# A projection's ends pinned in program order, and the C B product of each group moved three gemms later

## The chip, the core and the metric

The kernel runs on one core of a Trainium2 chip. Five engines work side by side: PE (TensorE) multiplies matrices into PSUM, DVE (VectorE) and ACT (ScalarE) do elementwise work, POOL (GpSimd) small copies, and SP (SyncE) issues most of the transfers. The metric is the device time of one execution in microseconds, the median of several runs. The profile shows one execution of its own.

## What is computed

One layer of a hybrid block on a sequence of 256 rows of width 2048, all in fp32: dilated attention with 16 heads beside a state-space (SSM) part with 8 groups of 8 heads, their branches gated, merged, projected and normalized. What matters here is the projection and the SSM part:

```python
hn = rms_norm(x, norm_w)
proj = hn @ w_in
q, k, v, z_a, z_s, xbc, dt_raw, g_a, g_s = jnp.split(proj, split_points, axis=-1)
...
xbc = jax.nn.silu(causal_depthwise_conv(xbc, conv_w, conv_b))
xs, bm, cm = jnp.split(xbc, [SSM_INNER, SSM_INNER + SSM_GROUPS * SSM_STATE], axis=-1)
dt = jax.nn.softplus(dt_raw.astype(jnp.float32) + dt_bias.astype(jnp.float32))
...
acum = jnp.cumsum(dac, axis=1)
decay = jnp.exp(jnp.where(causal, seg, -jnp.inf))
cb = jnp.einsum('blgn,bsgn->bgls', cc, bc)
y_diag = jnp.einsum('bgls,bgjls,bsgjp->blgjp', cb, decay, xc)
```

The kernel treats the two chunks of 128 rows as one triangle of three blocks, so that no state is carried: C B is made once for a group and multiplied by the decays of its eight heads.

## The kernel before

**Weights.** All weights stream once, in units of 128 x 1024 (L267 to L281). Of each unit ACT makes the rounded part `h` (L276) and DVE the rest `l` (L277); four of each are buffered. The activations XT lie there as a high and a low half side by side.

**Projections.** `gemm_a` (L320 to L333), called by `project`, makes one tile of 128 output columns over 16 steps `kt`. Each step has one product of `h` with both halves of XT (512 columns, L329) and one of `l` with the high half (256 columns, L332): 32 products in one PSUM bank. `gates` uses another form, `gemm_b`.

**Order.** The program is traced in one order, and a scheduler then orders the instructions of each engine anew, by priority and by when it takes each to be ready. Only what goes through `in_order` (`keep_in_program_order`, L200) is fixed: that instruction stays behind the last one traced before it on its engine. Before the change that holds for the products of the scan (L819).

**Ticks.** Each gemm begins with a `tick` (L316). `after(n, f)` puts a piece of work n ticks on. It runs when that gemm's tick comes, ahead of its first product; with a last argument of 1 it runs half a tick later, at L331, between the first and the second product of the gemm. What is due together runs in the order of due times.

**The SSM part.** In front come a first block of four tiles (`gemm_first`, four ticks), dt (one tick) and two gates of four ticks each. Then each group g has the gemms B and C (not group 0) and four times `xs` and `zs` (group 0 has three of each here, xs1 to zs3). What stands between:

- `dt_chain` (L704), on DVE, some thirty dependent small steps from dt_raw to the running sum `ac_t` (two scans, L733), all in the tile `early`. It is put nine ticks behind dt. When it runs it puts `dt_turn` (L737) DT_LAG = 2 ticks on: four transposes `dt_tp` (L742), the copies dtT and acT (L743, L744) and a product `lastb` (L746) that reads acT.
- `make_cb` (L766): the C B product of a group, in two products of plain fp32 (L768, L769, two passes each), and its masking on DVE (L770). It is put CB_LAG ticks behind the group's C, half a tick in; for group 0 at a place of its own (L890).
- `decays` (L772): ACT makes the decays of a group from `acb` and acT, DVE multiplies by cb (L791).
- `turn` (L793): eight transposes `xtp` (L801) of the group's `xs`, TURN_LAG = 3 ticks behind its last `xs`; that is in front of the next group's C.
- `scan` (L811): 16 products `yp` (L820, two passes each), half a tick into a later gemm. For group g that gemm is the last `zs` of group g + 1. `gather` (L828) follows on DVE and ACT.
- `conv`, `evac` and `half_silu` end each projection on ACT and DVE (L761, L383, L385, L387, L396, L397).

**The attention** uses `gemm_a` for q, k and za of 16 heads; `scores`, `turn_p` and `mix` come by ticks.

Of the kernel before, what the change touches and what calls it, by code (L numbers as in the profile page):

```python
# [16 lines left out]
S = 256  # L17
# [6 lines left out]
KT = D // P  # L24
# [9 lines left out]
X_CUTS = ((0, 1), (1, 2), (2, 4), (4, 6), (6, 8), (8, 10))  # L34
N_FINE = 4
N_ACT_X = 1
DT_LAG, CB_LAG, TURN_LAG, GT_LAG, Y_LAG, S_LAG, M_LAG = 2, 5, 3, 2, 11, 2, 2
Y_AFTER = 0, 0
GS_BEFORE = {0: (0, 1), 4: (2,)}
A_ORDERS = {0: (0, 1, 2, 4, 3, 6, 5, 7), 2: (0, 2, 1, 4, 3, 5, 6, 7)}  # L40
# [156 lines left out]
def hybrid_block(ctx: ExitStack, tc: tile.TileContext, wall, xt, x, pk_d, cst_d, fw_d, out):  # L197
    nc = tc.nc
    ve, ac, gp, pe = nc.vector, nc.scalar, nc.gpsimd, nc.tensor
    in_order = tc.keep_in_program_order  # L200
# [23 lines left out]
    def bank(tag, bufs, name):  # L224
        return ps.tile([P, 512], F32, name=name, tag=tag, bufs=bufs)
# [41 lines left out]
    def unit(n, shape):  # L267
        if n not in loaded:
            load(n)
        w = loaded.pop(n)  # L270
        h = stream.tile([P, UNIT], F32R, name=f"h{n}", tag="h", bufs=H_BUFS)
        l = stream.tile([P, UNIT], F32R, name=f"l{n}", tag="l", bufs=H_BUFS)
        cuts = (0, UNIT // 2, UNIT) if n < N_FINE else (0, UNIT)
        with tc.high_priority(L_AHEAD) if n >= KT // UB else nullcontext():
            for a, b in zip(cuts, cuts[1:]):
                ac.activation(h[:, a:b], w[:, a:b], AF.Copy)  # L276
                ve.tensor_tensor(l[:, a:b], w[:, a:b], h[:, a:b].bitcast(F32), ALU.subtract)  # L277
        for f in on_unit.pop(n, ()):
            f(h[:, 0:1].bitcast(F32))
        k, m = shape  # L280
        return h.rearrange("p (k m) -> p k m", k=k), l.rearrange("p (k m) -> p k m", k=k)  # L281
# [25 lines left out]
    def run_due(until):  # L307
        while True:
            ready = [d for d in due if d[0] <= until]
            if not ready:  # L310
                break
            d = min(ready, key=lambda e: e[0])
            due.remove(d)
            d[1]()

    def tick(final=False):  # L316
        now[0] += 1
        run_due(float("inf") if final else now[0])

    def gemm_a(tag, xs_of, acc=None):  # L320
        tick()
        name = f"{tag[0]}{tag[1]}"
        acc = bank(acc, 2, f"ps_{name}") if acc else bank("g", 4, f"ps_{name}")
        for u in range(KT // UK):
            h, l = unit(FIRST[tag] + u, (UK, P))
            for kk in range(UK):
                kt = u * UK + kk
                m = xs_of(kt)
                pe.matmul(acc, h[:, kk, :], m, start=(kt == 0), stop=False)  # L329
                if kt == 0:  # L330
                    run_due(now[0] + 0.5)  # L331
                pe.matmul(acc[:, S:], l[:, kk, :], m[:, :S], start=False, stop=(kt == KT - 1))  # L332
        return acc  # L333

    def gemm_dt(src):
# [23 lines left out]
    def project(tag, acc=None):  # L359
        return gemm_a(tag, lambda kt: XT[:, kt, :], acc)  # L360
# [324 lines left out]
    with tc.tile_pool(name="ssm", bufs=2) as sp:  # L685
# [223 lines left out]
        for g in range(GROUPS):  # L909
# [9 lines left out]
            for t in range(max(4 * g, 1), 4 * g + 4):  # L919
                u, i = divmod(t, 2)  # L920
                acc = project(("xs", t))
# [19 lines left out]
                acc = project(("zs", t))  # L941
# [330 lines left out]
```

## Time and profile before

| what | us |
|---|---|
| median of 3 runs | 1385.39 |
| lowest, highest | 1384.93, 1388.81 |
| span of the profiled execution | 1383.8 |
| PE busy in it | 1373.6 |
| DVE busy | 1169.5 |
| ACT busy | 835.5 |

The profiled execution's own time is its span, from the first to the last instruction, 1383.8 us. A row of the timeline gives the start in us, the time taken in us, engine, line, operation, the tile written and the tiles read, shapes and a count. Matmuls overlap in the pipeline: the distance of two starts is what a product costs, the time in its row is longer. A plain fp32 product shows as two matmuls. A row of the windows gives a stretch, its length, the busy time of each engine asked for with the number of instructions, the granted clock of PE, the share of the DMA engines and GB/s. A row of the groups gives the count, then busy time and mean duration in ns, then the idle time of the engine ahead of them with what ended it.

### The profile page before, as it was taken

How to read it: one execution, taken by the hardware profiler on the slowest of the kernel's cores; microseconds unless marked ns; L12 is line 12 of the kernel's file. 1: busy time of each engine (PE TensorE's matmuls, PEld its weight loads, DVE VectorE, ACT ScalarE, POOL GpSimd, SP SyncE). 2: the span in 40 equal slices, each digit the busy share in tenths (PEclk: the TensorE clock that was granted, in tenths of full speed). 3: DMA queues.
4: the chain of work that ended last, by engine and by line, in shares of the span. 5: the costliest groups of instructions: out<-in, count | busy, mean ns of one | idle time of the engine just before them, and what ended most of it. 6: DMA issues, size and time to landing. Idle time of an engine off the chain costs nothing.

```text
span 1383.8 us, 20696 instructions
## 1 busy us (share of the span) xinstructions
PE 1373.6 (99%) x7266; PEld 1169.9 (85%) x7266; DVE 1169.5 (85%) x1753; ACT 835.5 (60%) x1306; POOL 142.0 (10%) x226
## 2 busy tenths in 40 slices
PE   9999999999999999999999999999999999999997
PEld 8888888888888888888888888888888888888886
DVE  7898999987799898789889897777877788888897
ACT  7656677675667675766565554544544556655564
POOL 2301111101011100010001001111111000000112
PEclk9999999999999999999999999999999999999999
DMA  9767988868787866668677668888888757865773
GB/s 347 231 187 225 313 254 291 279 224 287 245 266 240 294 212 208 188 224 280 230 259 267 222 209 278 275 275 273 299 288 301 241 161 264 294 222 180 243 273 122
DMA packets 105080, 345.00 MB, mean 249 GB/s; under 512 B 11728, under 2 KB 13712, under 8 KB 104976
## 3 DMA queue, kind: packets, MB, share of 16 engines
q1 hardware_dynamic: 103536, 339.62, 74.0%
q10 hardware_dynamic: 1440, 4.06, 0.8%
q8 instruction: 57, 0.93, 0.3%
q14 instruction: 47, 0.39, 0.1%
HBM read 314.87 MB, written 28.77 MB: 248 GB/s over the span
## 4 chain that ended last, share of the span: by engine, by line
PE 97%; DMA 1%; DVE 1%; ACT 1%; issue 0%; SPq 0%; POOL 0%; POOLq 0%; DVEq 0%; ACTq 0%
PE ps_zs L329 8%; PE ps_xs L329 8%; PE ps_zs L332 4%; PE ps_q L329 4%; PE ps_za L329 4%; PE ps_k L329 4%; PE ps_xs L332 4%; PE ps_ssm L476 3%; PE ps_ssm L477 3%; PE ps_ssm L478 3%; PE ps_q L332 2%; PE ps_k L332 2%; PE ps_za L332 2%; PE ps_gs L414 2%; PE ps_gs L412 2%; PE ps_gs L413 2%
## 5 line engine op out<-in xcount | busy, mean ns | idle before, releaser
L276 ACT ACTIVATE h<-w 128x1024 fp32r<-128x1024 f32 (+1 forms) x398 | 413.9, 1047 | 318.0 <-issue 78.8
L277 DVE TENSOR_TENSOR l<-w,h 128x1024 fp32r<-128x1024 f32 (+1 forms) x398 | 479.4, 1211 | 124.2 <-ACT h L276 121.8
L329 PE MATMUL ps_zs<-XT,h 128*128 128x512 f32 x496 | 176.3, 397 | 0.0
L329 PE MATMUL ps_xs<-XT,h 128*128 128x512 f32 x496 | 175.9, 396 | 0.0
L332 PE MATMUL ps_zs<-XT,l 128*128 128x256 f32 x496 | 139.9, 282 | 0.0
L332 PE MATMUL ps_xs<-XT,l 128*128 128x256 f32 x496 | 139.8, 282 | 0.0
L329 PEld LDWEIGHTS ps_xs<-XT,h 128*128 128x128 f32 x496 | 93.3, 188 | 21.7
L329 PEld LDWEIGHTS ps_zs<-XT,h 128*128 128x128 f32 x496 | 93.4, 188 | 21.2
L332 PEld LDWEIGHTS ps_zs<-XT,l 128*128 128x128 f32 x496 | 93.7, 189 | 1.5 <-issue 0.7
L332 PEld LDWEIGHTS ps_xs<-XT,l 128*128 128x128 f32 x496 | 93.7, 189 | 0.4
L329 PE MATMUL ps_q<-XT,h 128*128 128x512 f32 x256 | 92.5, 405 | 0.2 <-ACT h L276 0.2
L329 PE MATMUL ps_k<-XT,h 128*128 128x512 f32 x256 | 89.9, 395 | 0.0
L329 PE MATMUL ps_za<-XT,h 128*128 128x512 f32 x256 | 89.7, 394 | 0.0
L543 ACT ACTIVATE ha<-wa 128x1024 fp32r<-128x1024 f32 x43 | 45.4, 1055 | 46.4 <-DMA wa<-in_wall 10.9
L332 PE MATMUL ps_q<-XT,l 128*128 128x256 f32 x256 | 71.2, 278 | 0.0
L332 PE MATMUL ps_k<-XT,l 128*128 128x256 f32 x256 | 71.1, 278 | 0.0
L332 PE MATMUL ps_za<-XT,l 128*128 128x256 f32 x256 | 71.1, 278 | 0.0
L544 DVE TENSOR_TENSOR la<-wa,ha 128x1024 fp32r<-128x1024 f32 x43 | 52.5, 1220 | 11.9 <-ACT ha L543 11.8
L782 ACT ACTIVATE gt<-acb,acT 128x128 f32<-128x128 f32 x128 | 44.2, 391 | 23.7 <-DMA acb<-acum_d 21.9
L329 PEld LDWEIGHTS ps_q<-XT,h 128*128 128x128 f32 x256 | 48.2, 188 | 11.5 <-ACT h L276 0.6
L329 PEld LDWEIGHTS ps_za<-XT,h 128*128 128x128 f32 x256 | 48.1, 188 | 11.3
L329 PEld LDWEIGHTS ps_k<-XT,h 128*128 128x128 f32 x256 | 48.1, 188 | 11.2
(688 smaller groups left out, 3325.1 us busy)
## 6 DMA issues: line engine op xcount, KB each, us to landing
w<-in_wall SPq DMA_DIRECT2D x394, 512.0 KB, 4.7
wa<-in_wall SPq DMA_DIRECT2D x43, 512.0 KB, 4.9
th_a<-in_wall SPq DMA_DIRECT2D x19, 512.0 KB, 5.6
sums_at<-in_wall SPq DMA_DIRECT2D x18, 512.0 KB, 4.7
acb<-acum_d SPq DMA_DIRECT2D x32, 256.0 KB, 4.0
t_ssm<-sums_at SPq DMA_DIRECT2D x13, 512.0 KB, 4.1
wt<-t_ssm SPq DMA_DIRECT2D x13, 512.0 KB, 5.4
th_a<-in_wall SPq DMA_DIRECT2D x19, 256.0 KB, 6.0
```

The source lines that it names most:

```text
L276: ac.activation(h[:, a:b], w[:, a:b], AF.Copy)
L277: ve.tensor_tensor(l[:, a:b], w[:, a:b], h[:, a:b].bitcast(F32), ALU.subtract)
L329: pe.matmul(acc, h[:, kk, :], m, start=(kt == 0), stop=False)
L332: pe.matmul(acc[:, S:], l[:, kk, :], m[:, :S], start=False, stop=(kt == KT - 1))
L412: pe.matmul(accs[i], xh, h[:, kk], start=(kt == 0), stop=False)
L413: pe.matmul(accs[i], xh, l[:, kk], start=False, stop=False)
L476: pe.matmul(acc, xh, h, start=start, stop=False)
L477: pe.matmul(acc, xh, l, start=False, stop=False)
L478: pe.matmul(acc, xl, h, start=False, stop=stop)
L543: ac.activation(h, src, AF.Copy)
L544: ve.tensor_tensor(l, src, h.bitcast(F32), ALU.subtract)
L782: ac.activation(g4[:, n, b], acb[:, j, b // 2 * P : b // 2 * P + P], AF.Relu, scale=-1.0, bias=sc[:, h : h + 1],)
```

## The change

CB_LAG goes from 5 to 8: the C B product of groups 1 to 7 is now due in the gemm in which the scan of the group in front is due, and is traced behind that scan. In `gemm_a` the first product (`h` of step 0) and the last (`l` of step 15) go through `in_order`. The first is so held behind the last PE instruction that was traced before it, which may be one of the tick's own; the last behind the product ahead of it.

```diff
-DT_LAG, CB_LAG, TURN_LAG, GT_LAG, Y_LAG, S_LAG, M_LAG = 2, 5, 3, 2, 11, 2, 2
+DT_LAG, CB_LAG, TURN_LAG, GT_LAG, Y_LAG, S_LAG, M_LAG = 2, 8, 3, 2, 11, 2, 2
...
                 m = xs_of(kt)
-                pe.matmul(acc, h[:, kk, :], m, start=(kt == 0), stop=False)
+                ends = [pe.matmul(acc, h[:, kk, :], m, start=(kt == 0), stop=False)]
                 if kt == 0:
+                    in_order(ends[0])
                     run_due(now[0] + 0.5)
-                pe.matmul(acc[:, S:], l[:, kk, :], m[:, :S], start=False, stop=(kt == KT - 1))
+                ends.append(pe.matmul(acc[:, S:], l[:, kk, :], m[:, :S], start=False, stop=(kt == KT - 1)))
+                if kt == KT - 1:
+                    in_order(ends[1])
```

## The prediction

> **What bounds the kernel now.** I read the page first: the engines, then the chain that ended last.
>
> ```profile
> span 1383.8 us, 20696 instructions
> ...
> PE 1373.6 (99%) x7266; PEld 1169.9 (85%) x7266; DVE 1169.5 (85%) x1753; ACT 835.5 (60%) x1306; POOL 142.0 (10%) x226
> ...
> PE 97%; DMA 1%; DVE 1%; ACT 1%; issue 0%; SPq 0%; POOL 0%; POOLq 0%; DVEq 0%; ACTq 0%
> ```
>
> The reader is to see that PE is never without work and that 97% of the last chain is PE. So an edit pays only if PE spends fewer microseconds on the same products, and any time for which PE is made to wait is lost whole: no slack anywhere absorbs it. A page that says 99% cannot show waits that do not exist yet. So next I went through the timeline of PE and, since the change fixes PE's order, that of the engines whose results PE would then have to wait for.
>
> **The C B products.** The timeline of PE, at the product of group 1 and at the scan of group 0:
>
> ```profile
> 146.87 0.59 PE L768 MATMUL cbp<-ct,bt 128*128 128x256 f32 x2
> 147.30 0.39 PE L769 MATMUL cbp<-ct,bt 128*128 128x128 f32 x2
> 147.65 0.39 PE L329 MATMUL ps_xs<-XT,h 128*128 128x512 f32 x1
> ...
> 164.24 0.40 PE L329 MATMUL ps_zs<-XT,h 128*128 128x512 f32 x1
> 164.57 2.82 PE L820 MATMUL yp<-gt,xdt 128*64 128x256 f32 x32
> 167.32 0.39 PE L332 MATMUL ps_zs<-XT,l 128*128 128x256 f32 x1
> 167.54 0.39 PE L329 MATMUL ps_zs<-XT,h 128*128 128x512 f32 x1
> ```
>
> From the first cbp to the next `h` product are 0.78 us, of which an `l` product would take 0.12 anyway (16 pairs take 5.54 in the window at 124.46 below, 0.35 a pair, and an `h` 0.23, 247.90 to 248.13): the detour costs 0.66 us. Its two passes over 256 columns take 0.43 (146.87 to 147.30), and two over 128, at half of that, 0.22: 0.65. So only some 0.01 us is a price of changing over and could be saved by standing elsewhere. The scan's detour is 164.24 to 167.54 less one `h` (0.23) and one `l` (0.12), 2.95 us; a change-over can be in it, at its end (0.22 for the `l` after it, not 0.12, and as much again before). If the C B product shared that end it would save up to 0.2 us a group, 1.4 for the seven groups 1 to 7; if passing from the scan's 64-column tiles to 128 costs a second time, it loses 0.1 each, 0.7. I take **0**, by the row of cbp itself, and keep −1.4 and +0.7. Nothing late follows on DVE: the result's first reader, L791 of the same group, comes two gemms (11 us) after the new place, and L770 (0.55 us) only moves.
>
> **The pace of the projections.** Gemms of 32 equal products do not all take equally long. The windows that hold one gemm each, one of each kind:
>
> ```profile
> 76.79:82.43 5.64, 5.64 (x16) 2.94 (x16) 1.00 0.60 193
> ...
> 124.46:130.00 5.54, 5.54 (x17) 3.00 (x17) 1.00 0.65 218
> ```
>
> 0.10 us apart at the same granted clock (1.00). Following the starts through the part, the pace changes only at interruptions. Behind each transpose (xtp) it is the short one; behind the cbp at 146.87 and those of groups 3 to 7 the long one; behind every scan the long one; and mostly also where the first product of a `zs` gemm stands inside the `xs` gemm before it:
>
> ```profile
> 247.90 0.40 PE L329 MATMUL ps_xs<-XT,h 128*128 128x512 f32 x1
> 248.13 0.39 PE L329 MATMUL ps_zs<-XT,h 128*128 128x512 f32 x1
> 248.37 0.28 PE L332 MATMUL ps_xs<-XT,l 128*128 128x256 f32 x1
> ```
>
> By those starts some 40 of the 70 gemms of groups 1 to 7 run at the long pace. The change takes the cbp away from the middle of the group and forbids the stray first product, so that only what stands between a scan and the next transposes (a `zs` and a `B`, some 12 gemms in all) should stay long. 28 gemms times 0.105: **−2.9 us**, between −4.2 (all 40) and +3.2 (the other 30 become long). Why the pace changes the trace does not show; I take it as a regularity. The Trainium skill, "TensorE: Matmul & The Clock Gate", "Wait — 56ns, not 53.3ns?", has a fixed 2.5 ns per matmul above N ÷ 2.4 GHz, whatever stood before; by it this term would be 0 and the sum 2.9 us higher, but the two kinds of window above disagree with a fixed gap.
>
> **The pinned products.** In front of `xs2` (the third `xs` tile, group 0) `tick` runs `dt_turn`: `dt_chain` is due nine ticks after the first gemms; the two gates take eight, so that is `xs1`, and DT_LAG is 2. `dt_turn` issues four transposes and then `lastb` (L746), which reads acT. Pinned behind the last PE instruction written before it, the first product of `xs2` will stand behind `lastb`. Now the transposes drift:
>
> ```profile
> 88.08 0.40 PE L329 MATMUL ps_xs<-XT,h 128*128 128x512 f32 x1
> ...
> 111.76 0.39 PE L329 MATMUL ps_B<-XT,h 128*128 128x512 f32 x1
> 112.08 0.33 PE L742 MATMUL dt_tp<-cst,early 64*128 64x64 f32 x2
> 112.35 0.70 PE L768 MATMUL cbp<-ct,bt 128*128 128x256 f32 x2
> ...
> 113.47 0.39 PE L332 MATMUL ps_B<-XT,l 128*128 128x256 f32 x1
> ...
> 118.78 0.33 PE L746 MATMUL lastb<-acT,cst 128*128 128x64 f32 x2
> 118.95 1.05 PE L801 MATMUL xtp<-cst,xs 128*128 128x128 f32 x8
> ```
>
> `xs2` starts at 88.08, `lastb` at 118.78, 30 us later. That is no idle choice of place, for DVE ends the chain late:
>
> ```profile
> 108.72 0.73 DVE L733 TENSOR_TENSOR_SCAN early<-early 64x128 f32<-64x128 f32 x2
> 109.38 1.19 DVE L277 TENSOR_TENSOR l<-w,h 128x1024 fp32r<-128x1024 f32 x1
> ...
> 114.22 0.28 DVE L743 COPY dtT<-dt_tp 128x128 f32<-128x128 f32 x1
> 114.41 0.28 DVE L744 COPY acT<-dt_tp 128x128 f32<-128x128 f32 x1
> ```
>
> So PE will stop at 88.08. Everything on PE is behind that product: the rest of `xs2`, and each later projection by its own pin. Only cbp of group 0 may go ahead. How long? While PE stands, DVE has less to do. DVE's windows, first the chain's tile `early` alone up to its end and up to 97.70, then all of DVE up to 97.70, and the groups of that stretch that need `xs2`:
>
> ```profile
> 88.10:109.50 21.40, 5.87 (x17) 1.00 0.67 189
> 88.10:97.70 9.60, 2.06 (x6) 1.00 0.66 187
> ...
> 88.10:97.70 9.60, 9.37 (x21) 1.00 0.66 187
> ...
> L277 DVE TENSOR_TENSOR l<-w,h 128x1024 fp32r<-128x1024 f32 x3 | 3.6, 1214 | 0.0
> ...
> L385 DVE TENSOR_TENSOR raw_x<-ps_xs,lo_x 128x256 f32<-128x256 f32 x1 | 0.4, 417 | 0.0
> ```
>
> The chain needs 5.9 us more of DVE in 17 dependent steps. Beside it DVE did 9.37 − 2.06 = 7.3 us; of these two of the three L277 (2.4) and L385 (0.4) wait for a buffer or a bank that only `xs2` frees, which leaves 4.5 us, plus L770 of the cbp that went ahead, 0.55. These gaps between dependent steps are filled one for one in the trace, so I count all of it: 88.1 + 5.9 + 4.5 + 0.5 = 99.0. Behind it come the last transposes (0.34), L743 and L744 (0.5), `lastb` and three handovers, some 0.5: 1.3. PE resumes at 100.2: **+12.1 us**. If the chain goes first it is 7.2.
>
> PE then restarts slow. The groups of the first 7.2 us, and PE's windows at the end of the run:
>
> ```profile
> L623 PE MATMUL warm<-ssq 128*128 128x256 f32 x8 | 3.8, 654 | 1.4 <-DVE ssq L620 1.4
> L377 PE MATMUL ps_first<-yTa,h 128*128 128x512 f32 x4 | 2.3, 718 | 0.0
> ...
> 1375.00:1379.50 4.50, 0.50 (x5) 1.00 0.71 260
> 1379.50:1383.80 4.30, 0.00 (x0) 0.50 0.60 215
> ```
>
> The granted clock falls to 0.50 some 4 us after the last matmul, and at the start products of 512 columns take 718 ns, not 400 (164.24), for the first 5.8 us (1.4 to 7.2). Half of 5.8 is 2.9; none if the few transposes in the stop keep the clock up. I take **+2.0**. The Trainium skill, "TensorE: Matmul & The Clock Gate", "What's actually happening", puts both the idle window and the slow restart at about 3.4 us; by that the term would be an estimated 1.7, and the sum 0.3 lower.
>
> In return the detours at 112.08 (113.47 − 111.76 less 0.23: 1.48) and of `lastb` at 118.78 (0.17) are gone from their old place, since they lie inside the stop: **−1.65**.
>
> The other pins bind little. Each C gemm is now behind the transposes of the group before, which need the last `xs`:
>
> ```profile
> 178.49 0.40 PE L329 MATMUL ps_C<-XT,h 128*128 128x512 f32 x1
> ...
> 178.15 0.42 DVE L397 SCALAR_TENSOR_TENSOR xs<-th_x,cv_x 128x256 f32<-128x256 f32 x1
> ...
> 824.90 0.50 PE L329 MATMUL ps_q<-XT,h 128*128 128x512 f32 x1 [0.20 <-ACT h L276]
> ...
> 824.90:832.90 8.00, 3.25 (x17) 1.00 0.85 291
> ```
>
> For group 1 that ends at 178.57, where C now begins at 178.49: some 0.2 us with the handover, and at most that in the six later groups. At 824.90 a product of the first q gemm fills a hole of the v gemm; pinned, it cannot, 0.3 us. The other q products in that window, all 17 together 3.25 us, stand among v's too, though no wait of v shows there. The attention's small products stand at gemm boundaries already. **+0.5**, from 0 to 4.6 (1.4 + 3.25).
>
> **Sum** against the profiled execution: 12.1 + 2.0 − 1.65 − 2.9 + 0.5 + 0 = +10.05; 1383.8 becomes 1393.85. The median is 1.6 us above that span, so the time is **1395.4 us**.
>
> **Rivals.**
> *The chain goes first.* DVE serves the 17 steps before the fillers (they were written earlier) and the clock holds: 7.2 − 1.65 − 2.9 + 0.5 = +3.2, 1388.6 us. For it: where no filler was ready (108.34 on) steps follow each other in 0.4 us. Against: up to 105 us each pair of steps has others between. 0.11.
> *No stop, faster.* The pin binds nothing long, because the chain is ended by the time `xs2` begins. It decides there: at 88.1 or before, the stop is nil. What stays is pace −2.9, the four gemms of group 0 short too −0.4, the shared end of the scan −1.4, pins +0.3: 1381.0 us. Against: 17 steps are left at 88.1, and nothing in the change touches what comes earlier. 0.14.
> *The pace does not follow.* The stop comes as forecast, but the long pace stays or spreads, by the skill's rule above 0 and at the far bound +3.2: with 0, 1398.3 us; up to 1401.5. 0.08.
> *The forecast*: 0.67.
>
> **The numbers.** A measurement here tells 0.3%, 4.2 us, from no change. Faster: 0.09 of the second rival. Same: its other 0.05 and 0.07 of the first, 0.12. Slower: 0.67, 0.04, 0.08, 0.79. The forecast's terms run from a stop of 7.2 to 13.5 and a pace of −4.2 to 0, so the range is 1386.5 to 1401; it takes in the first rival and most of the third and leaves out the second and the tails, 0.2.
>
> **What would show it.** In the profile after: PE idle before the first product of `xs2` for some 12 us, released by DVE or by `lastb`, with dt_tp and lastb right before it and DVE's L733 near 99; a granted clock under 1.00 there; cbp right behind yp with no gap and no saving; C, `xs` and `zs` at 5.55 a gemm, `zs` and `B` behind the scan at 5.65. No idle PE at 88 would fell the forecast; a stop with gemms still at 5.65 would fell the pace term alone.

## The result and the profile after

| | before | after |
|---|---|---|
| median of 4 runs, us | 1385.7 | 1398.74 |
| lowest, highest | 1384.93, 1388.81 | 1398.64, 1400.24 |
| span of the profiled execution | 1383.8 | 1397.0 |

The kernel became slower: the ratio of after to before is 1.0095, with an interval from 1.0081 to 1.0109. The forecast of 1395.4 had the sign and the main cause; the span grew by 13.2 us where the sum said 10.05. (In the changed kernel the `l` product's line is L333, not L332, and every line behind `gemm_a` has a number higher by three: L742, L746, L768, L801, L820 are now L745, L749, L771, L804, L823.)

The page of the changed kernel, engines, the clock in 40 slices, and the chain that ended last:

```profile
span 1397.0 us, 20700 instructions
...
PE 1373.7 (98%) x7266; PEld 1169.3 (84%) x7266; DVE 1171.0 (84%) x1753; ACT 837.9 (60%) x1306; POOL 148.5 (11%) x226
...
PEclk9989999999999999999999999999999999999999
```

PE has the same busy time as before, 1373.7 against 1373.6 us, in a span 13 us longer. That is misleading on its own, since slow products count as busy: a gain in one place and a loss in another cancel in the sum. The third slice, with a clock of 8 tenths, says where to look first. The timeline of PE there (start, duration, engine, line, operation, tiles, and in brackets the idle time in front with its releaser):

```profile
88.00 0.28 PE L333 MATMUL ps_zs<-XT,l 128*128 128x256 f32 x1
97.94 0.44 PE L745 MATMUL dt_tp<-cst,early 64*128 64x64 f32 x2 [9.65 <-DVE early L730]
98.31 1.22 PE L771 MATMUL cbp<-ct,bt 128*128 128x256 f32 x2
99.32 0.64 PE L772 MATMUL cbp<-ct,bt 128*128 128x128 f32 x2
99.89 0.47 PE L745 MATMUL dt_tp<-cst,early 64*128 64x64 f32 x2
101.00 0.69 PE L749 MATMUL lastb<-acT,cst 128*128 128x64 f32 x2 [0.64 <-DVE acT L747]
101.45 0.77 PE L329 MATMUL ps_xs<-XT,h 128*128 128x512 f32 x1
...
130.76 0.28 PE L333 MATMUL ps_B<-XT,l 128*128 128x256 f32 x1
133.82 1.10 PE L804 MATMUL xtp<-cst,xs 128*128 128x128 f32 x8 [2.78 <-DVE xs L400]
134.67 0.48 PE L329 MATMUL ps_C<-XT,h 128*128 128x512 f32 x1
```

There are **two stops**. The first is the forecast one: the stream of products ends at 88.12 (88.00 and the 0.12 of an `l`), and `xs2` starts at 101.45, behind `lastb`, 13.3 us later. The second was not forecast: 2.95 us between the end of the B gemm of group 1 (130.88) and the transposes of group 0's `xs`, behind which the C gemm of group 1 is now pinned.

The end of the chain on DVE:

```profile
98.21 0.73 DVE L736 TENSOR_TENSOR_SCAN early<-early 64x128 f32<-64x128 f32 x2
...
100.66 0.28 DVE L747 COPY acT<-dt_tp 128x128 f32<-128x128 f32 x1
```

It ends at 98.94, where the forecast had 99.0. From there to `xs2` it takes 2.5 us, not 1.3: PE serves the C B product of group 0 between the two halves of the transposes, from 98.31 to 99.89, and at half clock (0.50 from 97.9 to 101.4).

The windows of the changed kernel (length, then busy time and instructions of PE, PEld, DVE, ACT and POOL, the granted clock, DMA share, GB/s), at both stops:

```profile
88.10:101.40 13.30, 3.01 (x12) 2.15 (x11) 11.48 (x32) 2.98 (x6) 0.23 (x2) 0.62 0.31 92
101.40:108.60 7.20, 7.20 (x34) 6.25 (x34) 1.45 (x2) 2.88 (x7) 0.00 (x0) 0.76 0.23 73
...
130.80:133.80 3.00, 0.24 (x2) 0.00 (x0) 3.00 (x6) 1.86 (x4) 0.10 (x1) 1.00 0.92 296
```

The second row is the gemm `xs2`: 7.20 us at a clock of 0.76, 1.65 more than a gemm at the short pace. The last row shows that a stop of 3 us leaves the clock at 1.00. PE is idle for 10.3 us of the first row (13.30 less 3.01) and for 2.8 of the last: that is the 13 us by which the span grew, and the slow products and the quicker ones cancel in the busy time.

What feeds the second stop is ACT. Its timeline, then that of DVE:

```profile
104.13 0.70 ACT L785 ACTIVATE gt<-acb,acT 128x128 f32<-128x128 f32 x2 [10.00 <-DMA acb<-acum_d]
...
109.05 0.70 ACT L785 ACTIVATE gt<-acb,acT 128x128 f32<-128x128 f32 x2 [2.04 <-DMA acb<-acum_d]
...
120.48 0.70 ACT L785 ACTIVATE gt<-acb,acT 128x128 f32<-128x128 f32 x2 [2.83 <-DMA acb<-acum_d]
```

```profile
123.34 1.23 DVE L277 TENSOR_TENSOR l<-w,h 128x1024 fp32r<-128x1024 f32 x1 [3.92 <-ACT h L276]
...
133.34 0.42 DVE L400 SCALAR_TENSOR_TENSOR xs<-th_x,cv_x 128x256 f32<-128x256 f32 x1
```

While PE stands at 88, ACT comes to the decays of group 0, which need `acb`, a transfer that starts only when the chain has written ac_t (SP stores it at 98.97 and issues the first `acb` at 100.95). ACT works in order, so the weights' `h` (L276) stand behind that wait; DVE then stands for `h` (3.92 us before 123.34), and the last `xs` of group 0 is done at 133.76. The transposes start at 133.82.

What the change won is in the scan and behind it. The timeline of PE at scan 0, then PE's windows of three gemms, `xs` of group 1, `B` behind scan 0 and `xs` of group 2:

```profile
179.97 0.40 PE L329 MATMUL ps_zs<-XT,h 128*128 128x512 f32 x1
180.30 2.82 PE L823 MATMUL yp<-gt,xdt 128*64 128x256 f32 x32
183.05 0.70 PE L771 MATMUL cbp<-ct,bt 128*128 128x256 f32 x2
183.58 0.39 PE L772 MATMUL cbp<-ct,bt 128*128 128x128 f32 x2
183.72 0.36 PE L333 MATMUL ps_zs<-XT,l 128*128 128x256 f32 x1
183.93 0.40 PE L329 MATMUL ps_zs<-XT,h 128*128 128x512 f32 x1
```

```profile
140.40:146.05 5.65, 5.65 (x35) 1.00 0.68 217
189.13:194.68 5.55, 5.55 (x34) 1.00 0.72 209
201.11:206.65 5.54, 5.54 (x34) 1.00 0.71 237
```

The joint detour is 183.93 − 179.97 less an `h` (0.23) and an `l` (0.12): 3.61 us, as before for scan and C B product apart (2.95 + 0.66). Standing together saves nothing. But the `B` gemm behind it (189.13) runs at the short pace, and so does `xs` of group 2 (201.11). The `xs` of group 1 (140.40) is still long: it follows the second stop.

### The profile page after: what moved, and what is told of

It reads as the page before. It is cut to its first block, busy times and chain, and to the rows that moved or that the text cites. A ratio compares the mean times of both kernels' runs of the same rounds, so it can differ in the third digit from the quotient of the medians.

```text
span 1397.0 us, 20700 instructions
## 1 busy us (share of the span) xinstructions
PE 1373.7 (98%) x7266; PEld 1169.3 (84%) x7266; DVE 1171.0 (84%) x1753; ACT 837.9 (60%) x1306; POOL 148.5 (11%) x226
## 4 chain that ended last, share of the span: by engine, by line
PE 94%; DVE 2%; DMA 1%; ACT 1%; issue 1%; SPq 0%; POOL 0%; POOLq 0%; ACTq 0%; DVEq 0%
PE ps_xs L329 8%; PE ps_zs L329 8%; PE ps_k L329 4%; PE ps_za L329 4%; PE ps_q L329 4%; PE ps_xs L333 4%; PE ps_zs L333 4%; PE ps_ssm L480 3%; PE ps_ssm L481 3%; PE ps_ssm L479 3%; PE ps_q L333 2%; PE ps_k L333 2%; PE ps_za L333 2%; PE ps_gs L416 2%; PE ps_gs L417 2%; PE ps_gs L415 2%
## 5 line engine op out<-in xcount | busy, mean ns | idle before, releaser
L276 ACT ACTIVATE h<-w 128x1024 fp32r<-128x1024 f32 (+1 forms) x398 | 414.3, 1049 | 310.3 <-issue 78.1
L333 PE MATMUL ps_zs<-XT,l 128*128 128x256 f32 x496 | 138.8, 280 | 0.0
L333 PE MATMUL ps_xs<-XT,l 128*128 128x256 f32 x496 | 138.7, 280 | 0.0
L333 PEld LDWEIGHTS ps_xs<-XT,l 128*128 128x128 f32 x496 | 94.1, 190 | 0.0
L333 PEld LDWEIGHTS ps_zs<-XT,l 128*128 128x128 f32 x496 | 93.4, 188 | 0.0
L333 PE MATMUL ps_q<-XT,l 128*128 128x256 f32 x256 | 71.1, 278 | 0.0
L333 PE MATMUL ps_k<-XT,l 128*128 128x256 f32 x256 | 71.0, 278 | 0.0
L333 PE MATMUL ps_za<-XT,l 128*128 128x256 f32 x256 | 71.0, 277 | 0.0
L547 DVE TENSOR_TENSOR ltu<-wa,htu 128x1024 fp32r<-128x1024 f32 x38 | 46.4, 1222 | 15.6 <-ACT htu L546 15.6
```

Of the source, the lines that this page charges most:

```text
L333: ends.append(pe.matmul(acc[:, S:], l[:, kk, :], m[:, :S], start=False, stop=(kt == KT - 1)))
L547: ve.tensor_tensor(l, src, h.bitcast(F32), ALU.subtract)
```

## The experiments

Theory **A**: the loss comes from the pin on `xs2`'s first product, through both stops, the second being a consequence of the first; the lag of the C B product costs nothing. Its rival **B**: the moved C B product brings a part of the loss, or the many other pins do. All ratios are to the kernel before on the same chip; one us is 0.07%.

### The lag alone

```diff
-DT_LAG, CB_LAG, TURN_LAG, GT_LAG, Y_LAG, S_LAG, M_LAG = 2, 5, 3, 2, 11, 2, 2
+DT_LAG, CB_LAG, TURN_LAG, GT_LAG, Y_LAG, S_LAG, M_LAG = 2, 8, 3, 2, 11, 2, 2
```

The kernel before, with only this.

> The change with its lag alone: CB_LAG 8, no pin in the projections. Theory A (the loss of 13.0 us is made by the pins: PE is held at xs2 behind lastb and at the first C behind the transposes): no stop, PE idle under 0.5 us between 76 and 150, and a time within 3 us of before (1383 to 1388), the difference being the pace of the gemms, 0.105 us for each that turns long or short. Theory B (the moved C B product costs, because it waits or makes others wait behind the scan): 1390 us or more. The detour of scan and C B product together should take 3.6 us as in the changed kernel.

Measured: 1385.87 us, ratio 1.0004 [0.9995, 1.0012]. No stop, and no gain. The lag is without fault, and also without use when alone. The timeline of PE shows one reason, at the C B product of group 1:

```profile
147.65 0.39 PE L329 MATMUL ps_xs<-XT,h 128*128 128x512 f32 x1
147.87 0.59 PE L768 MATMUL cbp<-ct,bt 128*128 128x256 f32 x2
148.31 0.38 PE L769 MATMUL cbp<-ct,bt 128*128 128x128 f32 x2
148.44 0.36 PE L332 MATMUL ps_xs<-XT,l 128*128 128x256 f32 x1
```

The scheduler draws it ahead of the scan (165.57) by 18 us, to its old place, since nothing pins it. In the six other groups it does stand behind the scan, and the pace is short there; but the stray first products of the next gemm are still there, and in four groups (3, 5, 6 and 7) the first of them is where the pace turns long again.

### The pins alone

The changed kernel with CB_LAG back at 5.

> The pins alone, CB_LAG back at 5. Theory A: the stop at xs2 of about 13.3 us and the slow restart of about 1.65 us stay, the second stop at the first C too (about 2.9 us): 1397 to 1401 us. Theory B: near before, 1384 to 1388. Besides: if the C B product is what turns the pace long, the gemms from xs2 of a group to its scan take 5.65 us here, and the time is 1 to 3 us above the changed kernel's 1398.7.

Measured: 1399.47 us, ratio 1.0101 [1.0088, 1.0115]. The loss is all in the pins. PE's timeline has the first stop as in the changed kernel (`xs2` at 101.73), and the second one, of 2.2 us (132.03 to 134.26). The window of the `B` gemm behind scan 0 is long, where it is 5.55 with the C B product in front:

```profile
189.35:195.01 5.66, 5.66 (x34) 1.00 0.60 200
```

So behind a scan alone the pace was long 7 times of 7, and behind scan and C B product short 7 times of 7. The difference of the two medians, 0.7 us, is less than their intervals. With the C B product back in the middle of the group, the gemms behind it run at the short pace in six of the seven groups (group 4 is the exception). The prediction read the C B product as turning the pace long; here it does so in one group of seven.

### The first product of xs2 free

```diff
-                    in_order(ends[0])
+                    if now[0] != 16:
+                        in_order(ends[0])
```

Tick 16 is `xs2`. One pin is taken out of the changed kernel.

> The changed kernel, but the first product of xs2 alone (tick 16) is not pinned. Theory A: the stop of 13.3 us, the restart's 1.65 us and, if the second stop is only a consequence of the first, its 2.9 us go, and the detours of dt_tp and lastb (1.65 us) come back elsewhere: 1398.7 - 13.3 - 1.65 - 2.9 + 1.65 = 1382.5 us, faster than before by the pace. If the second stop is a cost of the pin at C by itself, 1385.4. Theory B (many pins each cost a little): above 1392.

Measured: 1382.3 us, ratio 0.9975 [0.9964, 0.9985]: with one of 124 pinned first products (31 `xs`, 31 `zs`, 14 `B` and `C`, 48 of the attention) taken out, the kernel is 16.4 us quicker than the changed one, and quicker than the one before. The timeline of PE has the transposes drifting again, 111.62 and 112.74, with no waits:

```profile
111.62 0.33 PE L746 MATMUL dt_tp<-cst,early 64*128 64x64 f32 x2
111.89 0.70 PE L772 MATMUL cbp<-ct,bt 128*128 128x256 f32 x2
112.42 0.38 PE L773 MATMUL cbp<-ct,bt 128*128 128x128 f32 x2
112.74 0.34 PE L746 MATMUL dt_tp<-cst,early 64*128 64x64 f32 x2
113.00 0.39 PE L334 MATMUL ps_B<-XT,l 128*128 128x256 f32 x1
```

The second stop is gone with the first, though the pin on C of group 1 still stands. The second is a consequence of the first.

### The stop filled with products

```diff
+            busy = bank("m2", 2, "busy")
+            for _ in range(N_BUSY):
+                in_order(pe.matmul(busy[:, :S], ssq[:, 0, :P], ssq[:, 0], start=True, stop=True))
```

Ahead of the transposes in `dt_turn`, with N_BUSY = 22.

> The changed kernel with 22 products more, of a tile of zeros, used for nothing, issued in front of the four transposes, so that PE works through the first 9.5 us of the stop instead of standing idle. Theory A with a price for the restart: the stop ends when it did or, since its last small products run at full clock, up to 1.5 us sooner, and xs2 takes 5.55 us and not 7.20: 1398.7 - 1.65 - 1.5 = 1395.6 us. If the slow restart is no matter of idleness: 1398.7. If the added products delay the transposes: above 1399.

Measured: 1401.42 us, ratio 1.0115 [1.01, 1.0131], a miss by 6 us. The windows of PE, DVE and the rest show that the first half of the expectation held and what went against it, `xs2` first, then the C gemm of group 1:

```profile
100.45:106.18 5.73, 5.73 (x34) 4.99 (x34) 0.22 (x1) 2.12 (x7) 0.00 (x0) 1.00 0.16 50
...
135.66:142.19 6.53, 6.53 (x35) 5.66 (x33) 3.75 (x7) 1.48 (x2) 0.10 (x1) 0.86 0.37 149
```

```profile
128.68 0.28 PE L334 MATMUL ps_B<-XT,l 128*128 128x256 f32 x1
134.04 1.97 PE L808 MATMUL xtp<-cst,xs 128*128 128x128 f32 x8 [5.07 <-DVE xs L401]
135.66 0.78 PE L330 MATMUL ps_C<-XT,h 128*128 128x512 f32 x1
```

With the clock kept up, the stop ended 1.0 us sooner and `xs2` took 5.73, not 7.20. But the release of the second stop did not move: 134.04, against 133.82. It is set by `acb`, ACT and DVE, not by PE, so all that PE won it spent waiting, 5.07 us now instead of 2.78, and that was long enough for the clock to fall (0.86 in the gemm behind it, and the transposes in 1.62 us instead of 0.85). Of the 2.7 us by which the span is longer than after, this gives 1.8 (0.2 later, 0.8 in the transposes, 0.8 in the gemm). The other 0.9 to 1.0 is lost late, in the v gemm: PE waits 0.53 us for an `h` of ACT before 839.46, a wait that the changed kernel does not have there, and the three products behind it take 0.95 us, not 0.69. Why that `h` comes late in this run is not shown.

### The first product of C of group 1 free

As in the third experiment, with `now[0] != 21`.

> The changed kernel, but the first product of the first C gemm alone (tick 21) is not pinned, so that the transposes of group 0 may drift into it; the pin at xs2 stays. Theory A (the second stop is a price of the pin at C, paid only because the first stop has pushed the last xs of group 0 late): the stop of 13.3 us stays, the 2.8 us of idle PE at 131 go, and the transposes come some products into C: 1398.7 - 2.8 = 1395.9 us. Rival (ACT stands at the decays, waiting for acb, and no more h and l arrive): PE waits as long for h or l of the C gemm, 1398 us or more.

Measured: 1395.96 us, ratio 1.0075 [1.0062, 1.0087]. The timeline of PE: the transposes are released as late as before, but C no longer waits for them.

```profile
133.81 0.40 PE L329 MATMUL ps_C<-XT,h 128*128 128x512 f32 x1
134.05 1.03 PE L805 MATMUL xtp<-cst,xs 128*128 128x128 f32 x8
134.84 0.36 PE L334 MATMUL ps_C<-XT,l 128*128 128x256 f32 x1
```

The span is 4.2 us shorter than after: the 2.95 of the stop, and most of the rest from the eight gemms behind it in group 1, which now run at the short pace (0.105 each, 0.8).

### Pins only from the first xs gemm of group 1 on

As above, with `now[0] >= 22`: no first product is pinned before the first `xs` of group 1.

> Pins only from tick 22 on, the first xs of group 1: neither xs2 nor the first C is pinned. If the pin at C costs nothing once the first stop is gone, as the run with xs2 alone free says (1382.3, its C waits for nothing), the same 1382.3 within 1 us. If the C pin has a price of its own, less than that by it.

Measured: 1382.38 us, ratio 0.9977 [0.9968, 0.9986], the same as with `xs2` alone free. No other pin of the early part costs anything by itself that these runs resolve; their intervals reach 1.2 to 1.5 us to each side.

### The transposes of dt four gemms later

```diff
-DT_LAG, CB_LAG, TURN_LAG, GT_LAG, Y_LAG, S_LAG, M_LAG = 2, 8, 3, 2, 11, 2, 2
+DT_LAG, CB_LAG, TURN_LAG, GT_LAG, Y_LAG, S_LAG, M_LAG = 6, 8, 3, 2, 11, 2, 2
```

All pins stand; the instruction they stand behind is traced later.

> The changed kernel with DT_LAG 6 instead of 2: all pins stay, but the transposes and lastb stand in front of the first B gemm (tick 20, near 110 us) and no longer of xs2. In the kernel before the running sum is ready at 109.5, so PE waits there for the last transposes, the copies and lastb alone, 1 to 3 us, too short for the clock to fall: 1382.3 + 1 to 3 = 1383.5 to 1385.5 us. If the pins cost by their number and not by this place: 1398.

Measured: 1383.53 us, ratio 0.9986 [0.9977, 0.9995]. PE's timeline, where `dt_turn` now is, in front of B of group 1:

```profile
110.82 0.28 PE L333 MATMUL ps_zs<-XT,l 128*128 128x256 f32 x1
111.03 0.46 PE L745 MATMUL dt_tp<-cst,early 64*128 64x64 f32 x4
112.07 0.43 PE L749 MATMUL lastb<-acT,cst 128*128 128x64 f32 x2 [0.58 <-DVE acT L747]
112.31 0.48 PE L329 MATMUL ps_B<-XT,h 128*128 128x512 f32 x1
```

1.4 us from the end of `zs3` (110.94) to the start of B, not 13.3: a pin of the same kind, behind an instruction whose input is nearly ready, is cheap.

### The transposes of xs pinned too

The sixth experiment, and `in_order(...)` around `pe.transpose` in `turn`. In the sixth, six of the eight transposes of group 3 floated into the gate in front of B of group 4, and only two stood before B, as in the changed kernel; that group's gemms then stayed long.

> Pins from tick 22 on, and the eight transposes of each turn kept together in program order, which puts those of group 3 in one piece in front of the B gemm of group 4. In the changed kernel two of them stand there and the nine gemms of group 4 up to its scan take 5.65 us each. If it is the full set of transposes in front of a gemm that makes the pace short, these take 5.55: 1382.3 - 0.95 = 1381.4 us. If the pace there has another cause: 1382.3.

Measured: 1381.7 us, ratio 0.9972 [0.996, 0.9983]. All eight now stand together, and the gemms of group 4 from B on are short: from B to the scan PE takes 50.33 us (314.63 to 364.96), in the sixth experiment 51.28 (314.92 to 366.20). That gain of 0.95 is what was expected; the two medians, 0.7 us apart, would not show it, since their intervals overlap. PE's timeline:

```profile
313.84 1.03 PE L805 MATMUL xtp<-cst,xs 128*128 128x128 f32 x8
314.63 0.47 PE L329 MATMUL ps_B<-XT,h 128*128 128x512 f32 x1
```

### All of it together

The eighth with DT_LAG = 6 and `in_order` around both products of `make_cb`, so that the C B product of group 1 can't float.

> What paid, together: pins from tick 22 on, the transposes of each turn and the two C B products of each group pinned too, DT_LAG 6. Against the run with the transposes pinned (1381.7) two things should turn the pace short: the C B product of group 0 alone in its gemm at 94 us (as with DT_LAG 6, three gemms, 0.3 us) and that of group 1 behind the first scan and no longer ahead of it (four and a half gemms, 0.45 us), with no wait at the first B gemm: 1381.0 us. If the pace does not follow the interruption in front of it: 1381.7 or more.

Measured: 1381.79 us, ratio 0.9973 [0.9962, 0.9983], 0.8 above the expectation, which is within the interval, and no better than the eighth. The pace was short from 95 us on and the C B product of group 1 stood behind its scan, as meant; but in an `xs` gemm PE then waited for weights:

```profile
150.08 0.39 PE L329 MATMUL ps_xs<-XT,h 128*128 128x512 f32 x1
151.00 0.39 PE L334 MATMUL ps_xs<-XT,l 128*128 128x256 f32 x1 [0.53 <-DVE l L277]
```

The `l` part came 0.5 us late, that gemm took 0.83 more than 5.55, and the pace behind it was long again up to the scan. At that place the limit was no longer PE's order but the supply from DVE.

## Why the prediction was right, and by how much it was short

Term by term, against the span (+13.2 us):

| term | forecast | measured |
|---|---|---|
| stop at `xs2` | +12.1 | +13.3 |
| slow restart | +2.0 | +1.65 |
| detours gone from their old place | −1.65 | −1.65 |
| pace, groups 1 to 7 | −2.9 | −2.4 |
| pace, four gemms of group 0 | not in the sum | −0.4 |
| C B product behind the scan | 0 | 0.0 |
| other pins | +0.5 | +2.95 − 0.4 |
| not separated | | +0.15 |
| sum | +10.05 | +13.2 |

- **The stop** came where it was put, by the pin that was named (the lag alone has none of it; the one pin taken out removes it), and the chain's end was right to 0.1 us. The rival by which the chain goes first is refuted, and so is the one without a stop. The 0.1 is in part luck. From 88.10 to 98.94 DVE is busy for 10.53 us, 5.94 with the chain and 4.59 with other work, much as forecast; but the masking of the C B product (0.55), counted in, came only behind the chain (99.99), and 0.3 us of gaps between steps stood in its place. The tail was 1.2 us short. It priced the C B product as done in front of the stop, on DVE only; on PE it stood between the two halves of the transposes, and at half clock.
- **The restart**: a gemm that runs at half rate for a time t loses t/2, so 1.65 us lost are 3.3 us at half rate, from 101.45 on. The kernel's own start showed 5.8, from which the 2.0 was taken. The Trainium skill, "TensorE: Matmul & The Clock Gate", "What's actually happening", puts the slow restart at about 3.4 us. The trace agrees if one counts from `xs2`; from the first product after the stop (97.94) the clock stays at half for 6.9 us more, with small products and a short wait in them. So 1.65 is one value of several: in two runs with the same stop `xs2` took 7.69 us (the pins alone) and 7.72 (the fifth experiment), 2.1 and 2.2 more than 5.55, and there the forecast's 2.0 is the nearer one.
- **The pace** followed, but by other gemms. The prediction left 12 gemms long, those between each scan and the next transposes. None of these was long once the C B product stood behind the scan. Long were 17 others: the eight of group 1 from C on, behind the second stop, and nine of group 4 from B on, where only two transposes stood in front. 40 − 17 = 23 times 0.105 is 2.4. Between scan 0 and scan 6 the traces show it directly: 385.21 us before, 382.52 after. One of the two reasons given in the prediction, that the C B product turns the pace long, does not hold in general (one group of seven in the second experiment), so it is partly luck that its count of gained gemms, 28, came near 23. The four gemms of group 0 behind the stop turned short too; the prediction has these −0.4 in its second rival alone. The Trainium skill's fixed gap per matmul ("TensorE: Matmul & The Clock Gate", "Wait — 56ns, not 53.3ns?"), by which the term would be 0, isn't borne out: the same 32 products took 5.55 and 5.65 us at a granted clock of 1.00 in one execution.
- **The step that was mis-sized** is that of the other pins, at most 0.2 us for each C gemm behind the transposes. The row that the prediction read, at 178.49, is the C gemm of group 2. At the C gemm of group 1, where the second stop came, the last `xs` was done 2.8 us ahead in the kernel before; DVE's timeline, then PE's:

```profile
114.61 0.42 DVE L397 SCALAR_TENSOR_TENSOR xs<-th_x,cv_x 128x256 f32<-128x256 f32 x1
...
117.86 0.39 PE L329 MATMUL ps_C<-XT,h 128*128 128x512 f32 x1
```

So no row of the trace before could show a wait there. The first stop itself changes that trace: it lets the decays of group 0 fall due before their `acb` has landed, ACT stands 10.0, 2.0 and 2.8 us, and the last `xs` is late. Size 2.95, and it is gone when `xs2` is free (third experiment) and when C is free (fifth). On the other side the passage from v to q was 0.4 shorter, not 0.3 longer: the v products up to 832.45 come 13.63 us later than before, the first k product (848.92) 13.21. The wait of 0.20 us for `h` ahead of the first q product is gone; that product still stands among v's, because the pin holds it only behind what was traced just before it.

The third rival, a stop with no gain in pace, would have given 1398.3 us, within half a us of the measured time. It is nonetheless not what happened: the gain in pace is there (2.4 us), and the second stop and the longer tail took it. That the two sums nearly meet is chance.

## What to carry to other kernels

A pin in program order turns the lateness of the instruction that it points at into a stop of all that follows on that engine; so for each pin, ask what its predecessor waits for, and when that is ready. Here one pin cost 16 us with what followed from it, and the rest of the change was worth 3: exempt that one or trace its predecessor later (the best version ran at 1381.7 us, ratio 0.9972 [0.996, 0.9983], by pins only from the first `xs` of group 1 on and with the transposes of `xs` pinned too; the third, sixth and ninth experiments lie within its interval). And once a stop is forecast, the rest of the trace before no longer holds behind it: walk the in-order queues (here ACT behind a transfer) once more with the times that the stop gives.

## What was not expected of the hardware

**Two paces.** The same stream of `h` and `l` products took 5.55 or 5.65 us a gemm, at the same granted clock, and kept its pace from one interruption to the next. Over the traces: long behind a scan alone (7 of 7 before, 7 of 7 with the pins alone), short behind scan and C B product (7 of 7 after), short behind eight transposes at a gemm's boundary where PE did not wait for them, long behind two waits of PE (the second stop; the late `l` of the ninth experiment) and mostly behind a stray first product of another gemm. Of these only three were switched by an edit: the C B product behind the scan, the second stop before group 1, and the two or eight transposes before group 4. The interruption alone does not settle it either. Behind the first stop, with the same instructions in front, the `zs` gemm after `xs2` took 5.55 us in the changed kernel and 5.54 in the fifth experiment, but 5.65 with the pins alone. Why the stream has two paces no run shows; it stays open.

**The clock and short stops.** 2.95 us without a matmul left the granted clock at 1.00, and 5.24 us took it to 0.86 over the next gemm. In the first stop, 9.8 us, it was at 0.50 from 91.3 us on, some 3 us after the last product, and stayed there until 104.8. In the two other runs with that stop the half rate lasted about as long, from 92.5 to 106.0 (the pins alone) and from 91.7 to 105.3 (the fifth experiment). How much of it falls on a full gemm differs with where the stop ends: 3.3 us of `xs2` in the changed kernel, 4.3 and 4.5 in the other two. At the start of the kernel before, the slow time was 5.8 us.
